# How many steps of projections stand between a normalised q or k tile and its transposes

## The chip, the cores and the metric

The kernel runs on one core of one Trainium2 chip. The metric is the device time of one execution in microseconds (us), taken as the median over several runs. The profile and the trace are of one such execution; its span runs from its first to its last instruction.

## What is computed

One decoder layer on 512 tokens of width 1024, in float32. Cut to what matters here:

```
h = rms_norm(x) * (1 + scale(c)) + shift(c)
proj = h @ w_in
(q_a, k_a, v_a, z_a, q_b, kc, vc, ks, vs, kw, vw, z_b, g_b) = split(proj)
qa, ka       = qk_norm(q_a) * qscale, qk_norm(k_a)
o_a          = sliding-window attention (window 128, sinks, bias), 8 heads, 2 kv heads
qb           = qk_norm(q_b) * qscale
k_cmp, v_cmp = two-layer MLP over overlapping blocks of kc, vc (k_cmp then qk-normed)
o_cmp        = softmax attention of qb on the compressed k_cmp, v_cmp
o_sel, o_win = attention of qb on qk_norm(ks), vs and on qk_norm(kw), vw, with bias
o_b          = gates * (o_cmp, o_sel, o_win), summed
y            = concat(o_a * silu(z_a), o_b * silu(z_b)) @ w_out ;  out = x + gate(c) * y
```

## The kernel before

TensorE works in float32 parts: a matrix is split into a high part and the rest (`wh`, `wl`; `hh`, `hl`), and a product of two matrices is three matmuls per contraction chunk. Heads are taken in pairs r = 0 to 3, one head of each of the two kv groups. Kind "a" is the sliding-window group, kind "b" the sparse one.

Two lines of work are interleaved from about 60 us on.

The first is `run()`, a list of slots of attention. A slot is one head pair, one branch and one block of 128 queries; there are 16 slots of kind a and then 28 of kind b. At turn t, `run()` writes the transposes of slot t-2 (`slot_trans`, L974 or L984), the scaling of slot t-1 (`slot_scale`), the scores of slot t (`slot_scores`, L923, or L896 for the slot that takes both branches of the first block), and, once a head pair is complete, its products with v (`slot_pv`, L1001). On TensorE these stand in blocks (`with block()`) that keep the order of the text among themselves.

The second is a stream of projections, a Python generator (`gen1`, then `gen2`). Each step of a unit writes three matmuls, for one contraction chunk (L503 in `unit_nat`, L513 in `unit_col`), and then yields a cost. `run()` draws steps from it by a budget of 3.6 us per turn for kind a (`PER_A`), half ahead of `slot_pv` and half behind it. Of the projections of kind b that matter here: the selected keys and values (`kv_sel`), the window's (`kv_win_g`), the queries in two halves (`q_b0`, `q_b1`, 96 matmuls each) and the gates' z units of 24 matmuls, z0 to z7.

What follows a projection is written as a small generator of its own and put in the list `posts`. `with_posts` takes one step of the first generator in that list after each step of projections. So a `yield 0.0` in such a generator puts one step of projections, three matmuls, between what is written before it and what is written after it. The generators that the change touches:

- `post_k(ty, kr)` normalises the keys of the selected (ty 1) and the window branch (ty 2): squares and sums, the eight small VectorE operations of `rsqrt`, and then `k_scale`: two VectorE multiplications into `kn` (L569, L571), two yields, four transposes into a PSUM tile `pt` (L576), and the copies and subtractions that split the transposed keys (L581, L582).
- `post_q(qr, half)` does the same for a half of the queries: sums (L542), `rsqrt`, and for each of its two head pairs `q_scale`: a multiplication into `qn` (L551), `Q_LEAD` = 3 yields, four transposes into `pt` (L557), two copies on ScalarE (L562) and two subtractions on VectorE (L563). Below, q0 to q3 are the four head pairs of kind b; q0 and q1 come from the first half, q2 and q3 from the second.

The keys of kind a (ty 0) and the queries of kind a go through the same two functions.

In `posts`, the keys of the selected branch stand ahead of `cmp_mlp`, the MLP of the compressed branch, whose first half of products (L630) is written by a step of it, and whose second half is written by `run()` at the next `slot_pv` (`jobs`). Its later steps hold a transpose of hidden values (L652), the second layer (L663, L666) and a transpose of the compressed keys `kcn` (L683). `cmp_attn` (L699 and on) comes after the queries and needs all four head pairs of them; its products stand in a block as well. `post_z` follows each z unit.

The text is not the order on an engine. The framework's planner goes through the text with its own estimates of durations, and gives each engine, at each moment, the earliest instruction of the text that it believes to be ready by then and that has room for its tile. The order so found is fixed in the program, and each engine then waits wherever an instruction is not ready.

Of the kernel before, what the change touches and what calls it, by code (L numbers as in the profile page):

```python
# [36 lines left out]
Q_LEAD = 3  # L37


def rev(ap):  # L40

    dims = [list(e) for e in ap.ap]
    step, n = dims[-1]
    dims[-1] = [-step, n]
    return bass.AP(tensor=ap.tensor, offset=ap.offset + step * (n - 1), ap=dims)
# [37 lines left out]
def hybrid_layer_kernel(ctx, tc, A, out):  # L83
# [11 lines left out]
    def T2(dt, name):  # L95
        return t2.tile([128, S], dt, name=name, tag="t2")
# [385 lines left out]
    def W2(name, shape=(128, 512)):  # L482
        return mp.tile(list(shape), F32, name=name, tag="w2", bufs=5)

    def PT():
        return ps_t.tile([128, 512], F32, name="pt")
# [48 lines left out]
    def sumsq(dst, src, nblk, on_act):  # L535
        sq = W2("sq")[:, 0:nblk * HD]
        if on_act:
            ACT.activation(sq.rearrange("p (a b) -> p a b", a=src.shape[1]) if len(src.shape) == 3 else sq,
                           src, AF.Square)
        else:  # L540
            POOL.tensor_tensor(sq, src, src, op=OP.mult)
        DVE.tensor_reduce(dst, sq.rearrange("p (b d) -> p b d", d=HD), AX.X, OP.add)  # L542

    def rnorm(ssq, n):
        DVE.tensor_scalar(ssq, ssq, 1.0 / HD, EPS, op0=OP.mult, op1=OP.add)
        return rsqrt(ssq, n)

    def q_scale(src, rn, heads):

        qn = W2("qn", (128, 8, HD))  # L550
        DVE.tensor_tensor(qn.rearrange("p (t h) d -> p t h d", t=NB), src,  # L551
                          rn[:, :, :, None].to_broadcast([128, NB, 2, HD]), op=OP.mult)
        for _ in range(Q_LEAD):
            yield 0.0
        pt = PT()
        for tb in range(NB):
            PE.transpose(pt[:, tb * 128:(tb + 1) * 128], qn[:, 2 * tb:2 * tb + 2].rearrange("p h d -> p (h d)"), ident)  # L557
        view = lambda ap: ap.rearrange("p (t q) -> p t q", t=NB)
        for n, h in enumerate(heads):
            qs[h] = T2(F32R, f"qs{h}")  # L560
            own, other = slice(64 * n, 64 * n + 64), slice(64 - 64 * n, 128 - 64 * n)
            ACT.activation(view(qs[h][own]), rev(view(pt[own])), AF.Copy)  # L562
            DVE.tensor_tensor(view(qs[h][other]), rev(view(pt[own])), view(qs[h][own]).bitcast(F32), op=OP.subtract)  # L563
        yield 0.44

    def k_scale(ty, src, rn):

        kn = W2("kn", (128, 8, HD))
        DVE.tensor_tensor(kn, src.rearrange("p t (g d) -> p (t g) d", d=HD), rn[:, :, None].to_broadcast([128, 8, HD]),  # L569
                          op=OP.mult)  # L570
        DVE.tensor_tensor(kn, kn, kg[:, ty:ty + 1, :].to_broadcast([128, 8, HD]), op=OP.mult)  # L571
        for _ in range(2):
            yield 0.0
        pt = PT()
        for t in range(NB):
            PE.transpose(pt[:, t * 128:(t + 1) * 128], kn[:, 2 * t:2 * t + 2].rearrange("p g d -> p (g d)"), ident)  # L576
        for g in range(2):
            own = slice(64 * g, 64 * g + 64)
            high = kT[ty, g][own, 0, :]
            for part in (own, slice(64 - 64 * g, 128 - 64 * g)):  # L580
                ACT.activation(kT[ty, g][part, 0, :], pt[own, :], AF.Copy)  # L581
                DVE.tensor_tensor(kT[ty, g][part, 1, :], pt[own, :], high.bitcast(F32), op=OP.subtract)  # L582
        yield 0.44
# [3 lines left out]
    def prep_a():  # L587
        ss = sm.tile([128, 40], F32, name="ss_a")
        for tb in range(NB):
            DVE.tensor_reduce(ss[:, 8 * tb:8 * tb + 8], qsq[tb].rearrange("p (b d) -> p b d", d=HD), AX.X, OP.add)  # L590
        DVE.tensor_reduce(ss[:, 32:40], ksq.rearrange("p t (g d) -> p (t g) d", d=HD), AX.X, OP.add)
        rn = rn_a[0] = rnorm(ss, 40)
        yield 0.0
        yield from k_scale(0, kraw, rn[:, 32:40])
        yield from prep_q_a(0)

    def prep_q_a(r):
        pair = lambda ap: ap.rearrange("p (t g r) -> p t g r", t=NB, g=2)[:, :, :, r]
        q4 = qraw.rearrange("p t (g r d) -> p t g r d", g=2, r=4)
        yield from q_scale(q4[:, :, :, r], pair(rn_a[0][:, 0:32]), (r, 4 + r))  # L600
# [176 lines left out]
    def post_k(ty, kr):  # L777
        ss = sm.tile([128, 8], F32, name="ss_k")
        sumsq(ss, kr.rearrange("p t n -> p (t n)"), 8, True)
        rn = rnorm(ss, 8)  # L780
        yield from k_scale(ty, kr, rn)
# [10 lines left out]
    def post_q(qr, half):  # L792

        ss = sm.tile([128, 16], F32, name="ss_q")
        for p in range(2):
            sumsq(ss[:, 8 * p:8 * p + 8], qr[:, 2 * p:2 * p + 2].rearrange("p t n -> p (t n)"), 8, True)
        yield 0.0
        rn = rnorm(ss, 16).rearrange("p (t h) -> p t h", t=NB)
        for j in range(2):
            r = 2 * half + j  # L800
            yield from q_scale(qr[:, :, 128 * j:128 * j + 128].rearrange("p t (g d) -> p t g d", g=2),
                               rn[:, :, 2 * j:2 * j + 2], (8 + r, 12 + r))

    def gen1():
        for _ in range(2):
# [23 lines left out]
        for half in range(2):  # L829
            qr = mp.tile([128, NB, 256], F32, name="pp", bufs=3)  # L830
            for p in range(2):
                b = PJ()
                yield from with_posts(unit_nat(f"q_b{half}", (2 * p, 2 * p + 1), 256, b))
                ACT.activation(qr[:, 2 * p:2 * p + 2, :], b.rearrange("p (t n) -> p t n", t=2), AF.Copy)
            posts.insert(0, post_q(qr, half))
# [318 lines left out]
```

## Time and profile before

| | us |
|---|---|
| median of 3 runs (lowest to highest) | 306.42 (305.98 to 307.14) |
| the profiled execution, its own time | 306.31 |
| its span | 304.2 |
| TensorE matmuls busy | 296.2 (97%) |
| TensorE weight loads busy | 251.6 (83%) |
| VectorE (DVE) busy | 238.3 (78%) |
| ScalarE (ACT) busy | 195.3 (64%) |

Times inside the execution are counted from the start of its span, so its own time is 2.1 us above the span. In a row of the timeline stand the start, the duration, the engine, the line of the kernel, the operation with what it writes and reads, and how many instructions the row joins; a wait ahead of it stands in brackets with what ended it. Matmuls overlap: one of 256 columns shows 0.28 us, but the next one starts 0.12 us after it. So a hold of TensorE is read from starts, not from busy time.

### The profile page before, as it was taken

To read this page: it belongs to the slowest core of one execution; us is meant where nothing else is said; L and a number is where in the kernel's file an instruction comes from. 1 tells how busy PE (TensorE), PEld (TensorE's weight loads), DVE (VectorE), ACT (ScalarE), POOL (GpSimd) and SP (SyncE) were. 2 spreads that over 40 slices of the span, in tenths; PEclk is the share of its full clock that TensorE was granted. 3 is DMA by queue.
4 is the path that set the end of the run, shared out by engine and by line. 5 is a ranking of instruction groups with operands and counts; after the bars stand their busy time and mean duration, and the time that the engine had idled before them with its cause. 6 is when DMAs were issued, how large, how long until landed. Compare 5 with 4: busy or idle time off the path is not lost.

```text
span 304.2 us, 5822 instructions
## 1 busy us (share of the span) xinstructions
PE 296.2 (97%) x2118; PEld 251.6 (83%) x2119; DVE 238.3 (78%) x669; ACT 195.3 (64%) x474; POOL 3.8 (1%) x26
## 2 busy tenths in 40 slices
PE   7899999999999999989999999999999999999995
PEld 3677888889999999989887688788878888787885
DVE  4889996999985596877899999999985985819211
ACT  4876547777886578859666767776866875824000
POOL 1000000000000000000000000000000000000000
PEclk9999999999999999999999999999999999999999
DMA  7999947887225960320682023236100000105301
GB/s 276 375 375 408 354 178 246 270 271 264 83 93 165 354 211 2 111 62 9 225 285 72 1 79 130 82 127 199 46 1 2 0 2 1 37 0 180 132 34 69
DMA packets 27419, 44.20 MB, mean 145 GB/s; under 512 B 1712, under 2 KB 19408, under 8 KB 27392
## 3 DMA queue, kind: packets, MB, share of 16 engines
q1 hardware_dynamic: 27392, 43.84, 42.4%
q8 instruction: 16, 0.26, 0.3%
q14 instruction: 11, 0.09, 0.1%
HBM read 41.70 MB, written 2.14 MB: 144 GB/s over the span
## 4 chain that ended last, share of the span: by engine, by line
PE 74%; DVE 12%; ACT 8%; DMA 3%; issue 2%; SPq 1%; POOL 0%; ACTq 0%; POOLq 0%
PE pj L513 28%; PE sq L299 8%; PE po L1001 8%; PE pj L503 6%; PE s L923 6%; PE skv L300 4%; PE pt L984 4%; PE pt L974 3%; DMA ada_ring<-in_w_ada_ss 3%; PE s L630 2%; ACT pa L938 2%; DVE wl L181 2%; DVE qs L563 1%; ACT wh L180 1%; DVE pa L931 1%
## 5 line engine op out<-in xcount | busy, mean ns | idle before, releaser
L503 PE MATMUL pj<-wh,hh 128*128 128x256 f32 (+1 forms) x128 | 36.9, 288 | 0.0
L181 DVE TENSOR_TENSOR wl<-raw,wh 128x512 fp32r<-128x512 f32 (+1 forms) x52 | 35.4, 690 | 1.4 <-PE pj L503 0.8
L503 PE MATMUL pj<-wl,hh 128*128 128x256 f32 (+1 forms) x128 | 36.5, 285 | 0.0
L503 PE MATMUL pj<-wh,hl 128*128 128x256 f32 (+1 forms) x128 | 36.4, 285 | 0.0
L180 ACT ACTIVATE wh<-raw 128x512 fp32r<-128x512 f32 (+1 forms) x52 | 31.1, 636 | 6.7 <-PE pj L513 4.4
L938 ACT ACTIVATE pp<-pp,nm 128x256 f32<-128x256 f32 (+2 forms) x48 | 29.3, 612 | 7.8 <-DVE nm L931 7.7
L513 PE MATMUL pj<-hh,wl 128*128 128x512 f32 x80 | 32.3, 404 | 0.0
L513 PE MATMUL pj<-hh,wh 128*128 128x512 f32 x80 | 32.1, 401 | 0.0
L513 PE MATMUL pj<-hl,wh 128*128 128x512 f32 x80 | 31.7, 396 | 0.0
L931 DVE CUSTOM_DVE_ANT_0 pp<-s,bias 128x256 f32<-128x256 f32 (+2 forms) x48 | 25.6, 552 | 4.0 <-PE s L923 3.7
L513 PE MATMUL pj<-yh,wl 128*128 128x512 f32 (+1 forms) x72 | 26.8, 373 | 0.0
L513 PE MATMUL pj<-yl,wh 128*128 128x512 f32 (+1 forms) x72 | 26.7, 371 | 0.0
L513 PE MATMUL pj<-yh,wh 128*128 128x512 f32 (+1 forms) x72 | 26.4, 371 | 0.0
L503 PEld LDWEIGHTS pj<-wl,hh 128*128 128x128 f32 x128 | 24.1, 189 | 0.4 <-issue 0.3
L503 PEld LDWEIGHTS pj<-wh,hh 128*128 128x128 f32 x128 | 24.1, 188 | 0.4 <-issue 0.3
L503 PEld LDWEIGHTS pj<-wh,hl 128*128 128x128 f32 x128 | 24.1, 188 | 0.0
L923 PE MATMUL s<-kTb,qs 128*128 128x256 f32 (+2 forms) x96 | 23.7, 359 | 0.0
L959 DVE TENSOR_SCALAR pp<-pp,rr,grev 128x256 f32<-128x256 f32 (+2 forms) x48 | 21.0, 476 | 0.5
L1080 DVE SCALAR_TENSOR_TENSOR fin<-pj,gate_lsb,xr 128x512 f32<-128x512 f32 (+1 forms) x9 | 6.2, 690 | 16.1 <-PE pj L513 16.1
L985 ACT COPY ptT<-pt 128x384 f32<-128x384 f32 (+1 forms) x32 | 15.7, 529 | 3.3 <-PE pt L984 3.3
L513 PEld LDWEIGHTS pj<-hl,wh 128*128 128x128 f32 x80 | 15.0, 188 | 3.2
L513 PEld LDWEIGHTS pj<-hh,wl 128*128 128x128 f32 x80 | 15.1, 189 | 2.9
(246 smaller groups left out, 703.5 us busy)
## 6 DMA issues: line engine op xcount, KB each, us to landing
ada_ring<-in_w_ada_ss SPq DMA_DIRECT2D x16, 512.0 KB, 9.7
raw<-in_w_cmp SPq DMA_DIRECT2D x8, 512.0 KB, 5.4
raw<-in_w_gate SPq DMA_DIRECT2D x8, 512.0 KB, 6.4
raw<-in_w_o SPq DMA_DIRECT2D x8, 512.0 KB, 3.8
wst_ring<-in_w_qkv_a SPq DMA_DIRECT2D x8, 384.0 KB, 9.4
bias<-line_d SPq DMA_DIRECT2D x8, 256.0 KB, 4.5
xr<-in_xT SPq DMA_DIRECT2D x8, 256.0 KB, 4.2
raw<-in_w_q_b SPq DMA_DIRECT2D x4, 512.0 KB, 5.6
```

Of the source, the lines that this page charges most:

```text
L180: ACT.activation(wh, src, AF.Copy)
L181: DVE.tensor_tensor(wl, src, wh.bitcast(F32), op=OP.subtract)
L299: PE.matmul(pj_q[tb], lt, w[:, 0:512], start=f, stop=l, skip_group_check=True)
L300: PE.matmul(pj_kv[tb // 2][:, tb % 2, :], lt, w[:, 512:768], start=f and tb % 2 == 0, stop=l, skip_group_check=True)
L503: PE.matmul(bank[:, t * n:(t + 1) * n], h[:, tb * 128:(tb + 1) * 128], w[:, k % 2, :], start=k == 0 and m == 0, stop=k == 7 and m == 2)
L513: PE.matmul(bank, w, h[:, cols], start=k == 0 and m == 0, stop=k == 7 and m == 2)
L923: PE.matmul(ps[g], qs[h][:, 128 * i:128 * i + 128], kT[br, g][:, hl_, lo:lo + n], start=hl_ == 0, stop=hl_ == 1)
L931: DVE.tensor_tensor_reduce(out=P[:, g, 0:w], in0=ps[g][:, 0:w], in1=bt, scale=1.0, scalar=init, op0=OP.add, op1=OP.min, accum_out=nm[:, g: ...
L938: ACT.activation(P[:, g, 0:e], P[:, g, 0:e], AF.Exp, bias=nm[:, g:g + 1], scale=-1.0, accum_out=dn[:, g:g + 1])
L959: DVE.tensor_scalar(v, v, rr[:, g:g + 1], gates[:, g, br:br + 1], op0=OP.mult, op1=OP.mult)
L985: ACT.copy(T[:, 0:nb, :], rev(pt[:, 0:nb * 128].rearrange("p (b q) -> p b q", b=nb)))
L1001: PE.matmul(o[64 * g:64 * g + 64, 128 * i:128 * i + 128], vb[:, 64 * g:64 * g + 64], sl["T"][g][:, b, :], start=first_of and b == 0, stop= ...
```

## The change

`q_scale` gets its number of yields as an argument. `post_q` gives it `Q_LEAD * (2 - j)`: six for the first head pair of each half (q0 and q2) and three, as before, for the second. In `k_scale` the number becomes four for the two key tiles of kind b and stays two for kind a. The queries of kind a keep three.

```diff
-    def q_scale(src, rn, heads):
+    def q_scale(src, rn, heads, lead=Q_LEAD):
...
-        for _ in range(Q_LEAD):
+        for _ in range(lead):
             yield 0.0
         pt = PT()
...
-        for _ in range(2):
+        for _ in range(4 if ty else 2):
             yield 0.0
         pt = PT()
...
             yield from q_scale(qr[:, :, 128 * j:128 * j + 128].rearrange("p t (g d) -> p t g d", g=2),
-                               rn[:, :, 2 * j:2 * j + 2], (8 + r, 12 + r))
+                               rn[:, :, 2 * j:2 * j + 2], (8 + r, 12 + r),
+                               Q_LEAD * (2 - j))
```

No instruction is added or removed. The second head pair of a half comes after the first in the same generator, so all that follows q0 or q2 in it moves by three steps; all that follows the selected keys in `posts`, `cmp_mlp` first, moves by two.

## The prediction

> **What bounds the kernel now.** I read the page first, then the windows, then the waits of TensorE, then its timeline around each of the transposes that move. The page gives the span and who carries the chain that ended last.
>
> ```profile
> span 304.2 us, 5822 instructions
> ...
> PE 74%; DVE 12%; ACT 8%; DMA 3%; issue 2%; SPq 1%; POOL 0%; ACTq 0%; POOLq 0%
> ```
>
> Three windows in the stretch that the change touches; the columns are the length, then busy time and count of PE, PEld, DVE, ACT and POOL, the granted clock, the DMA share and GB/s.
>
> ```profile
> 130.00:140.00 10.00, 8.83 (x80) 8.52 (x80) 8.34 (x25) 6.52 (x17) 0.38 (x2) 1.00 0.09 33
> 150.00:160.00 10.00, 9.88 (x56) 8.14 (x55) 9.63 (x33) 5.32 (x17) 0.00 (x0) 1.00 0.77 262
> 170.00:200.00 30.00, 29.91 (x160) 24.58 (x159) 29.18 (x86) 22.13 (x54) 0.00 (x0) 1.00 0.27 89
> ```
>
> PE is full nearly everywhere, at a granted clock of 1.00; 130 to 140 is the exception, with 1.17 us idle. From 150 on DVE is nearly full too. The waits of PE, all together, name one wait on a q tile:
>
> ```profile
> PE pt L557 <- DVE qn L551: 1.2, 1, 1.2
> ```
>
> In the timeline of PE that wait stands at q0.
>
> ```profile
> 130.47 0.28 PE L503 MATMUL pj<-wl,hh 128*128 128x256 f32 x1
> 130.59 0.28 PE L503 MATMUL pj<-wh,hl 128*128 128x256 f32 x1
> 132.04 0.63 PE L557 MATMUL pt<-first,qn 128*128 128x128 f32 x4 [1.17 <-DVE qn L551]
> 132.42 0.37 PE L503 MATMUL pj<-wh,hh 128*128 128x256 f32 x1
> 132.62 0.60 PE L557 MATMUL pt<-first,qn 128*128 128x128 f32 x4
> 133.06 0.60 PE L974 MATMUL pt<-first,pa 128*128 128x128 f32 x4
> ```
>
> Matmuls start 0.12 us apart; from 130.59 to 132.04 it is 1.45, so 1.33 us of PE is lost. As PE carries 74% of the chain, a lost microsecond here counts nearly whole. The other moved transposes, k1 and k2 (selected, window) and q2 and q3, and that of `kcn`, stand here:
>
> ```profile
> 89.85 0.29 PE L503 MATMUL pj<-wh,hl 128*128 128x280 f32 x1
> 89.98 0.29 PE L503 MATMUL pj<-wh,hh 128*128 128x280 f32 x1
> 90.40 0.63 PE L576 MATMUL pt<-first,kn 128*128 128x128 f32 x4
> 90.86 0.38 PE L974 MATMUL pt<-first,pa 128*128 128x128 f32 x2
> ...
> 108.39 0.33 PE L683 MATMUL pt<-first,kcn 128*128 128x128 f32 x1
> 108.55 0.60 PE L974 MATMUL pt<-first,pa 128*128 128x128 f32 x4
> ...
> 152.43 0.39 PE L513 MATMUL pj<-hh,wh 128*128 128x512 f32 x1
> 152.66 0.40 PE L513 MATMUL pj<-hl,wh 128*128 128x512 f32 x1
> 153.18 0.66 PE L557 MATMUL pt<-first,qn 128*128 128x128 f32 x4
> 153.67 0.60 PE L974 MATMUL pt<-first,pa 128*128 128x128 f32 x4
> 154.03 0.72 PE L896 MATMUL s<-kTb,qs 128*128 128x256 f32 x4
> 154.59 0.60 PE L557 MATMUL pt<-first,qn 128*128 128x128 f32 x4
> ```
>
> At k1 PE loses 0.42 less 0.13, so 0.29 us; at q2 0.52 less 0.23, again 0.29. These three holds, 1.91 us, are all that later transposes of k1, q0 and q2 could win on PE.
>
> **Where the transposes stand, in the text and in the program.** This decides the case. The windows below begin with the first matmul of a unit and end at the transposes; the count in brackets is that of the projections' matmuls in between: `kv_win_g` ahead of k1, `q_b0` ahead of k2, `q_b1` ahead of q0, z0 ahead of q2.
>
> ```profile
> 80.03:90.30 10.27, 8.41 (x61) 1.00 0.40 128
> 106.42:114.20 7.78, 4.76 (x38) 1.00 0.64 208
> 125.32:131.00 5.68, 4.80 (x39) 1.00 0.69 209
> 144.00:153.00 9.00, 8.95 (x38) 1.00 0.66 216
> ```
>
> Now the places in the text, three matmuls a step. k1: `kn` in step 1 and two yields, so transposes in step 3, behind 9 matmuls; with four yields behind 15. k2: the gates take steps 1 and 2, so behind 15, after the change 21. q0: sums in step 1, `qn` in step 2, three yields, so step 5 and 15 matmuls; with six yields step 8 and 24. q1: `qn` in the step after q0's transposes, three yields, so 27, then 36. q2 as q0: 15, then 24. q3: 33, then 42, as `post_z` of z0 takes two steps in between.
>
> So the program does not have them where the text has them: 61 against 9 at k1, 38 against 15 at k2, 39 against 15 at q0, 38 against 15 at q2. The planner had already put them at the point at which it believed them ready, 23 to 52 matmuls later. The new places, 15, 21, 24 and 24, are still earlier than that. The longer lead is a lower bound that was overrun already, and should move none of these four. The 1.33 us at q0 is then an error of the planner's estimate, not a short lead: it believed `qn` ready at about 130.7, and DVE ended it at 131.9 (1.29 us for two of them from 131.20, so 0.65 for the first).
>
> ```profile
> 126.76 0.57 ACT L834 ACTIVATE pp<-pj 128x512 f32<-128x512 f32 x1
> ...
> 131.20 1.29 DVE L551 TENSOR_TENSOR qn<-pp,n_y 128x512 f32<-128x512 f32 x2
> ...
> 134.69 1.41 DVE L563 TENSOR_TENSOR qs<-pt,qs 64x512 fp32r<-64x512 f32 x2
> ```
>
> The chain from the copy of the projection (126.76) to `qn` is untouched by the edit. I cost q0, k1, k2 and q2 at 0.
>
> **What the change does move.** First, q3: its place was behind 38 matmuls (none stands between q2's and q3's transposes) and may not be earlier than 42 now. Four matmuls at 0.23 us (152.43 to 152.66) make it 0.9 us later. Nobody on PE waits for q3 before `cmp_attn`, priced below. q1's place, 40, stays allowed (36).
>
> Second, slot blocks pass transposes. Behind k1, `kcn`, q1 and q2 a slot's transposes (L974) start at once (90.86, 108.55, 133.06, 153.67), in every case a slot written later than the transposes ahead of it. I read this as slots held in text order behind late transposes. With about 11 steps a turn (3.6 us at 0.33 us of cost), turn 13 is written behind 30 matmuls of `q_b1`, turn 16 behind 15 to 18 of z0, turn 17 behind 33. Before, q1 (27), q2 (15) and q3 (33) were written ahead of these turns; after, they come behind them (36, 24, 42). `kcn` likewise falls behind turn 7. So four blocks of transposes and scores stop waiting for a transpose written after them: turn 13 by the 0.44 us of q1's transposes (132.62 to 133.06); turn 16 by up to 20 matmuls of z0 (38 less 18), 4.7 us; turns 7 and 17 something between. For PE this is an exchange, a block earlier and projections later, and worth 0 by itself. But their VectorE and ScalarE work starts earlier, in front of a stretch in which DVE is 97% busy (29.18 of 30). The bounds: no gain, and the removal of the small holds that PE still has at slot transposes in the stretch behind, for which q2's 0.29 is the nearest row; six slots so held would be 1.7 us. I take one such hold, 0.3 us, since PE is at 29.91 of 30 there and shows little to win.
>
> Third, the loads. `cmp_mlp` calls eight loads on SP's queue with its products, two steps later in the text (6 matmuls of 0.13 us, 0.8 us). The products stood in the program behind k1 and its slot, after 61 matmuls of `kv_win_g`; their new text place, 13 steps or 39 matmuls, is still earlier, so the loads go out when they did. Cost 0; without that cover 0.8 us of lateness on a queue that moves 33 GB/s in 130 to 140. The first half of the products must be written before the `slot_pv` of head pair 0, as the second half is written there: it was step 11 of `kv_win_g` and is now step 13, and that half turn draws to step 14 or so. It fits by one step; if it did not, the second half would come four turns later.
>
> The sum, against the profiled execution's own 306.31: 0 for q0, k1, k2, q2; 0 for q3; -0.3 for the slots: **306.0 us**. The median of the runs, 306.42, is 0.1 above the profiled execution, less than their spread.
>
> **The rivals.** (1) The planner moves the transposes along with the text: its readiness shifts by as much as the lead, and the holds at k1, q0 and q2 go. Then 306.31 - 1.91 = **304.4**, with the slots' 0.3 even 304.1. For it: the hold at q0 is real and is the largest of PE in the touched stretch. Against it: the counts, 39 against 24.
>
> (2) Slower, at `cmp_attn`. Its products need q3's last subtraction, and they stood behind it with room:
>
> ```profile
> 162.95 0.69 DVE L563 TENSOR_TENSOR qs<-pt,qs 64x512 fp32r<-64x512 f32 x1
> ...
> 167.44 1.06 PE L699 MATMUL s<-qs,kTc 128*32 128x512 f32 x8
> ```
>
> That is 163.64 to 167.44, 3.8 us. Now q3 is written behind two slots and z0's post, and DVE is full there (9.63 of 10). If the planner puts L699 where it believes q3 ready, its error decides. At q0 that error was 1.33 us on a chain of 5.1 (126.76 to 131.9), a quarter; q3's chain from its transposes to its last subtraction is 9.05 us (154.59 to 163.64), a quarter of it 2.4 us, with PE and all slot blocks behind it held. Then 306.0 + 2.4 = **308.4**. It decides from the point at which L699 is next on PE before q3's last subtraction has ended; 3.8 us of room, and nine matmuls by which L699 also moves in the text, speak against it.
>
> (3) A hold for want of a PSUM bank. The pool of `pt` names two banks; q0's is read until the subtractions that start at 134.69 (1.41 us for two), so up to 136.1. If the slot transposes had to wait for it behind 133.06, up to 3.0 us could go: **309.0**. Against it: at 133.06 a third `pt` tile was written while q0's and q1's were still unread. The Trainium skill, in Perfetto Trace Analysis under Optimization Strategy, says that one gap that repeats on the engine that should be full can mean that PSUM or SBUF lacks room for the next tile. By that rule the holds at k1, q0 and q2 would be one shortage, and slots closer to the q transposes would make it worse, to this rival's 309.0. The trace disagrees at 133.06, and names `qn`, not a reader of `pt`, as what ended the hold.
>
> **How the numbers follow.** Half a per cent is 1.5 us, about what a measurement of this kernel can tell from no change. The main case, the holds stay and the slots bring 0 to 1.7 us, gets 0.62, of which 0.04 lies below 304.8. Rival 1 gets 0.20, all faster; rival 2 gets 0.14 and rival 3 0.04, all slower. So faster 0.24, the same 0.58, slower 0.18. The range runs from rival 1 with a little on top, 304.1, to two thirds of rival 2's price with the slots' gain lost, 306.3 + 1.6 = 307.9. The main case alone: 304.6, all of the 1.7 won, to 306.9, nothing won and two new holds like k1's.
>
> **What would show it.** Right: in the trace after, q0's transposes stand behind 39 matmuls of `q_b1`, give or take 3, with a hold on `qn` of 1 us or more; k1 and k2 behind about 61 and 38; L974 and L896 of turns 16 and 17 come ahead of q2 and q3; q3 stands behind 42 or more of z0. Wrong: q0 without a hold, or behind fewer or many more matmuls; a new wait of PE on L563 at L699; a wait of L974 on a reader of `pt`. What would make it wrong most easily is that a small shift of the text makes the planner arrange the stretch from 100 us on anew, as its errors, and so the holds, then fall elsewhere.

## The result and the profile after

| | us |
|---|---|
| after, median of 11 runs (lowest to highest) | 308.46 (307.12 to 308.95) |
| before, median of 11 runs beside them | 306.07 (305.71 to 307.14) |
| ratio | 1.0072 [1.0057, 1.0087] |
| profiled execution of after, its span | 308.59, 306.5 |

The change makes the kernel slower by 0.72%, some 2.2 us. The forecast was no change, 306.0, with a range that ended at 307.9. In the kernel after, the lines up to 801 keep their numbers and those behind are one higher (L1002 is L1001 of before). The page gives the span and the chain that ended last.

```profile
span 306.5 us, 5856 instructions
...
PE 60%; DVE 23%; DMA 7%; ACT 5%; issue 2%; SPq 2%
```

TensorE carried 74% of that chain and carries 60% now; VectorE and DMA have taken the rest. So something outside TensorE has got onto the path. The waits of PE say where.

```profile
PE pt L576 <- DVE kn L571: 1.1, 2, 0.9
PE po L1002 <- DVE nm L932: 1.0, 1, 1.0
PE pt L557 <- DVE qn L551: 0.8, 1, 0.8
...
PE s L924 <- ACT kT L581: 0.4, 1, 0.4
```

The third line is the hold at q0, known from before and even smaller. The longer of the two waits in the first line and the wait in the second make up most of the loss, and neither stands at an instruction that the edit moves. The first of them in the timeline of PE, before and then after:

```profile
61.14 0.40 PE L513 MATMUL pj<-hh,wl 128*128 128x512 f32 x1
61.39 0.66 PE L576 MATMUL pt<-first,kn 128*128 128x128 f32 x4
```

```profile
61.43 0.40 PE L513 MATMUL pj<-hh,wl 128*128 128x512 f32 x1
62.76 0.33 PE L576 MATMUL pt<-first,kn 128*128 128x128 f32 x1 [0.94 <-DVE kn L571]
```

These are the transposes of kind a's keys, whose two yields the edit leaves alone. Before, they stood 0.25 us behind the matmul ahead of them, now 1.33. So 1.1 us is lost at 62 us, and the order of instructions is the same in both programs, on every engine that computes, up to about 101 us. A delay that comes ahead of the first instruction in another order can't come from the order. It leads back through `kn` and ScalarE to a load. The queue of SP, the engine that issues the loads, first before and then after; the duration of a pair reaches to the end of its second issue:

```profile
35.93 0.33 SPq L429 DMA_DIRECT2D rest<-in_rest  x1
36.35 9.94 SPq L161 DMA_DIRECT2D raw<-in_w_kv_cmp  x2
```

```profile
43.04 0.33 SPq L429 DMA_DIRECT2D rest<-in_rest  x1
43.46 3.13 SPq L161 DMA_DIRECT2D raw<-in_w_kv_cmp  x2
```

The load of `rest` (480 KB of small constants) goes out 7.1 us later. What it waits for is in the list of waits of that queue, and what comes of it on ScalarE in the timeline:

```profile
SPq L429 <- DVE xTp L283: 6.2, 1, 6.2
```

```profile
51.92 1.67 ACT L180 ACTIVATE wh<-raw 128x512 fp32r<-128x512 f32 x3 [1.10 <-DMA raw<-in_w_kv_cmp]
```

L283 is the last scaling of the input by `rb`. `rest` and `rb` have nothing to do with each other in the kernel's text, but the framework places all tiles in SBUF by itself from their lifetimes. In the built program after, `rest` lies at bytes 114464 to 119328 of a partition and `rb` at 114464 to 116512. `rest` had the same place before; it is `rb` that has moved, from byte 189408, and before no tile of that time shared the place of `rest`. So the load must wait for the last reader of `rb`, and the load of `kv_cmp` queued behind it waits too. ScalarE splits that weight (L180) ahead of the copies from which `kn` is made. Before, the same three splits began without a wait:

```profile
50.47 1.66 ACT L180 ACTIVATE wh<-raw 128x512 fp32r<-128x512 f32 x3
```

The second loss is at the first product with v of head pair b0. PE after, and then DVE after:

```profile
203.68 0.94 PE L924 MATMUL s<-kTb,qs 128*128 128x384 f32 x4
204.47 0.40 PE L513 MATMUL pj<-hh,wl 128*128 128x512 f32 x1
205.89 0.44 PE L1002 MATMUL po<-ptT,vs 128*64 128x128 f32 x4 [1.03 <-DVE nm L932]
```

```profile
203.44 1.26 DVE L248 CUSTOM_DVE_ANT_0 raw<-raw,scb,first 128x1024 f32<-128x1024 f32 x1
...
204.63 0.73 DVE L960 TENSOR_SCALAR pp<-pp,rr,grev 128x256 f32<-128x256 f32 x2
205.28 0.55 DVE L932 CUSTOM_DVE_ANT_0 pp<-s,bias 128x384 f32<-128x384 f32 x1
```

In both programs `po` of b0 is put into the PSUM bank of the first of the two score tiles written just ahead of it, so its first matmul waits until VectorE has read those scores (L932). After, the planner has a row sum for the gate (L248, 1.26 us, needed only at the end of the kernel) and a slot's scaling on VectorE ahead of that read, and one projection matmul on TensorE to cover it. Before, three matmuls stood there on PE, and on VectorE the read came ahead of the row sum. PE before, and then DVE before:

```profile
201.16 0.95 PE L923 MATMUL s<-kTb,qs 128*128 128x384 f32 x4
...
202.42 0.40 PE L513 MATMUL pj<-hl,wh 128*128 128x512 f32 x1
202.74 0.44 PE L1001 MATMUL po<-ptT,vs 128*64 128x128 f32 x4
```

```profile
201.79 0.56 DVE L931 CUSTOM_DVE_ANT_0 pp<-s,bias 128x384 f32<-128x384 f32 x1
...
203.46 1.28 DVE L248 CUSTOM_DVE_ANT_0 raw<-raw,scb,first 128x1024 f32<-128x1024 f32 x1
```

### The profile page after: what moved, and what is told of

Read it like the earlier page. It is cut to its first block, busy times and chain, and to the rows that moved or that the text cites. A ratio compares the mean times of both kernels' runs of the same rounds, so it can differ in the third digit from the quotient of the medians.

```text
span 306.5 us, 5856 instructions
## 1 busy us (share of the span) xinstructions
PE 296.8 (97%) x2119; PEld 252.1 (82%) x2119; DVE 238.5 (78%) x669; ACT 197.1 (64%) x474; POOL 4.6 (1%) x26
## 4 chain that ended last, share of the span: by engine, by line
PE 60%; DVE 23%; DMA 7%; ACT 5%; issue 2%; SPq 2%
PE pj L513 26%; PE po L1002 8%; PE s L924 7%; PE pj L503 6%; DVE ada_ring L248 4%; PE pt L985 4%; DMA wst_ring<-in_w_qkv_a 4%; PE pt L975 3%; DVE wl L181 3%; PE s L630 2%; DMA raw<-in_w_kv_cmp 2%; DVE swl L278 2%; DVE pa L932 1%; DMA ada_ring<-in_w_ada_ss 1%; ACT wh L180 1%
## 5 line engine op out<-in xcount | busy, mean ns | idle before, releaser
L180 ACT ACTIVATE wh<-raw 128x512 fp32r<-128x512 f32 (+1 forms) x52 | 31.9, 639 | 19.0 <-PE pj L513 13.7
L513 PE MATMUL pj<-hl,wh 128*128 128x512 f32 x80 | 32.1, 401 | 0.0
L513 PE MATMUL pj<-hh,wl 128*128 128x512 f32 x80 | 31.9, 399 | 0.0
L513 PE MATMUL pj<-hh,wh 128*128 128x512 f32 x80 | 31.9, 398 | 0.0
L932 DVE CUSTOM_DVE_ANT_0 pp<-s,bias 128x256 f32<-128x256 f32 (+2 forms) x48 | 25.5, 551 | 3.1 <-PE s L924 3.0
L513 PE MATMUL pj<-yl,wh 128*128 128x512 f32 (+1 forms) x72 | 26.9, 374 | 0.0
L513 PE MATMUL pj<-yh,wl 128*128 128x512 f32 (+1 forms) x72 | 26.7, 371 | 0.0
L513 PE MATMUL pj<-yh,wh 128*128 128x512 f32 (+1 forms) x72 | 26.2, 370 | 0.0
L513 PEld LDWEIGHTS pj<-hh,wh 128*128 128x128 f32 x80 | 15.0, 188 | 3.1 <-ACT qraw L472 0.2
L513 PEld LDWEIGHTS pj<-hh,wl 128*128 128x128 f32 x80 | 15.0, 188 | 3.1
L513 PEld LDWEIGHTS pj<-hl,wh 128*128 128x128 f32 x80 | 15.1, 188 | 2.9 <-issue 0.2
```

The source lines that it names most:

```text
L180: ACT.activation(wh, src, AF.Copy)
L513: PE.matmul(bank, w, h[:, cols], start=k == 0 and m == 0, stop=k == 7 and m == 2)
L932: DVE.tensor_tensor_reduce(out=P[:, g, 0:w], in0=ps[g][:, 0:w], in1=bt, scale=1.0, scalar=init, op0=OP.add, op1=OP.min, accum_out=nm[:, g: ...
```

## The experiments

Theory L: the loss is a new SBUF layout (the late load) plus the new order on VectorE at b0. Rival T: the longer leads, and the order that they make, cost it. Rival C: the hold at b0 is a consequence of something else, and taking it away brings nothing. Ratios below are to the kernel before, timed beside each run (305.7 to 305.9 us).

**Taking away the shared place, and splitting the change.** The first three runs have one edit in common, which keeps `rest` alive from the start:

```diff
     rest = con.tile([128, 1216], F32, name="rest")
+    POOL.memset(rest[:, 0:1], 0.0)
```

In the file the write stands on the line above it, behind a semicolon, so in the kernels below the lines keep the numbers of before (L1001, not L1002). The whole change with it:

> The change as it stands, and one write of zeros into a column of `rest` by GpSimd at the start, so that no early tile can share the place of `rest` in SBUF. TensorE, VectorE and ScalarE get the same instructions in the same order as after the change; only what the load of `rest` (L429) waits for differs. Theory L (the layout: `rest` was put over `rb`, so its load and the loads of `kv_cmp` behind it on SP's queue went out 7.1 us later): the load goes out at about 36 instead of 43.04, the transposes of kind a's keys come at 61.4 to 61.7 instead of 62.76, and the time falls by 1.1 to 1.4 us, from 308.46 to 307.1 to 307.4; the hold of 1.03 us at L1001 (b0) stays, since the order is the same. Rival T (the longer leads and their order cost it all): 308.4, no change. Rival C (the hold at b0 is only a consequence of the early delay): both go, 306.1.

Measured: 306.90 us, ratio 1.0035 [1.0020, 1.0050].

```profile
35.73 0.33 SPq L429 DMA_DIRECT2D rest<-in_rest  x1
```

```profile
PE po L1001 <- DVE nm L931: 1.1, 1, 1.1
```

The queue of SP has the load back at 35.7 and PE's waits still have the hold at b0. By PE's timeline the transposes of kind a's keys stand at 61.56. 0.37%, 1.1 us, is won with the same order on PE, VectorE and ScalarE. T falls for this half.

The two parts of the change alone, `4 if ty else 2` in `k_scale` and `Q_LEAD * (2 - j)` in `post_q`:

> The keys' part of the change alone (four steps for the two key tiles of kind b; the queries keep three and three), with `rest` written early as in the run before, so that its place is not shared. The order differs from before only in 51 matmuls between k2's projections and `cmp_mlp`. Theory L: nothing is lost, 306.1 (305.8 to 306.5). Rival T, if the keys' order carries the loss: 307.2 or more, with a shift that begins between 85 and 125 us.

Measured: 305.19 us, 0.9978 [0.9967, 0.9990]. Not only is nothing lost, 0.6 to 0.7 us is won against before, which no theory had; this median is the lowest of the study.

> The queries' part alone (six steps for q0 and q2), with `rest` written early so that its place is not shared. Theory L: no loss up to 190 us; the hold at L1001 of head pair b0 belongs to the order that this part makes, so about 1.0 us is lost there: 307.1 (306.8 to 307.4). Rival T: 308.4, the whole loss. Rival C: 306.1, no hold at b0.

Measured: 307.10 us, 1.0040 [1.0026, 1.0054], with the hold of 1.0 at L1001. As L had it.

> The queries' part alone without that early write; here the load of `rest` again waits for VectorE, as after the change. TensorE, VectorE and ScalarE have the same order as in the run before (queries alone, kept apart). Theory L: 1.1 to 1.4 us above that run, about 308.4, the difference made before 63 us. Rival T: the same time as that run.

Measured: 308.50 us, 1.0077 [1.0059, 1.0095], 0.37% above the run before. The load goes out at 42.3. By the ratios the price of the shared place is the same 1.1 us in two pairs of equal order.

**Making the load late by hand.** The best kernel so far, the keys' part with `rest` apart, gets the wait back without any shared place. `LW` moves the load two steps later in the text, behind the second write:

```diff
-LW = 4
+LW = 6
...
             DVE.tensor_tensor(y[k][:, c], xT[k][:, c], by[:, c], op=OP.mult)
+            k == 7 and DVE.memset(rest[:, 0:1], 0.0)
```

> The keys' part alone with `rest` apart, and a second write of zeros into a column of `rest`, by VectorE right behind the last scaling by `rb` (L283), ahead of the load in the text (which moves from step 3 to step 5 of the first stage for that). All engines keep the order of the keys' part alone; only the load of `rest` waits for that write, so it goes out at about 42.7 instead of 35.4, as after the change. Theory L: the lateness alone costs 1.1 us: 306.3 (306.0 to 306.6) against 305.19 of the keys' part apart, made at kind a's key transposes, 61.3 to about 62.4. Rival (the late load is only a companion of something else in the new layout): 305.2, no difference.

Measured: 306.25 us, 1.0010 [0.9997, 1.0023], so 1.06 us above 305.19 (0.98 by the ratios). PE shows the same wait at the same place as after the change:

```profile
61.81 0.66 PE L576 MATMUL pt<-first,kn 128*128 128x128 f32 x4 [0.91 <-DVE kn L571]
```

With that write some 2 us earlier on VectorE, behind L292 for chunk 5, and so the load at 39.67:

> The same with the second write behind the high-low split of chunk 5 (L292), so that the load of `rest` goes out at about 40 instead of 35.4. After the change the loads of `kv_cmp` were 7.1 us late and ScalarE waited 1.1 us for them beyond a moved chain of its own, so theory L has some 5 to 6 us of room: 4.5 us of lateness cost nothing, 305.2 (304.9 to 305.5). Rival (each microsecond of lateness costs its share, 1.1 for 7.1): 305.9.

Measured: 305.38 us, 0.9976 [0.9965, 0.9987]. Against the load of the keys' part (35.43), 4.3 us of lateness cost nothing that can be told from noise, and 6.5 us (41.95; 7.2 if counted against TensorE, which ran 0.7 us earlier in that execution) cost 1.06: it isn't a price per microsecond but a room that runs out. The windows show where; the last two columns are the DMA share and GB/s, first in the kernel before, then with the load at 41.95.

```profile
36.00:43.00 7.00, 7.00 (x43) 6.13 (x42) 6.93 (x14) 4.29 (x8) 0.00 (x0) 1.00 0.82 279
46.00:52.00 6.00, 6.00 (x33) 5.01 (x32) 3.48 (x6) 4.29 (x8) 0.00 (x0) 1.00 0.75 225
```

```profile
36.00:43.00 7.00, 7.00 (x42) 6.13 (x41) 6.96 (x12) 4.85 (x8) 0.00 (x0) 1.00 0.37 127
46.00:52.00 6.00, 6.00 (x34) 5.17 (x33) 2.44 (x4) 3.21 (x6) 0.00 (x0) 1.00 0.93 313
```

The second load of `kv_cmp` waits for a place of its own and is not late: it goes out at 45.74 before and at 44.95 here. What the late load does is move `rest` and the first half of `kv_cmp`, 992 KB, out of a stretch at 0.82. The larger part goes into 43 to 46 us, where nothing was moved before (0 GB/s, 256 here), and the rest falls behind 46 us, where the DMA engines go to 0.93 against 0.75 before and 0.78 with the load at 39.67. ScalarE then waits for both halves: 0.85 us ahead of the first split (L180), at 47.80, and 1.17 us ahead of the next three, at 50.97, which began at 50.40 without a wait when the load stood at 39.67. That the fuller stretch is what delays the second half is read from these rows; no run changed it alone.

**Other leads.** Five steps for q0 and q2 in place of six, keys four, `rest` apart:

> Queries with five steps for q0 and q2 instead of six, keys with four, `rest` apart. In this program six matmuls of projections and more stand on TensorE between the last scores of b0 and its first product with v, where six steps leave one; the piece of the gate's row sum (L248, 1.27 us) comes on VectorE behind the first reduction of those scores instead of ahead of it. Theory L (the hold of 1.03 us at L1001 is the price of that order): no hold at L1001 of b0, and about 0.9 us below the change with `rest` apart (306.9): 306.0 (305.5 to 306.4). Rival C (the longer lead of the queries costs by itself, or the fuller SBUF places of `wh` cost it): 306.9 or more, without a hold at L1001.

Measured: 308.90 us, 1.0091 [1.0071, 1.0110]. A miss. The hold at b0 did go down to 0.2, but a new one stands behind the last head pair:

```profile
275.62 0.39 PE L1007 MATMUL po<-ptc,vc_low 128*128 128x512 f32 x1
277.45 0.73 PE L513 MATMUL pj<-yh,wh 128*128 128x512 f32 x2 [1.44 <-ACT yh L860]
```

The matmuls of projections that cover b0 there are missing later. Their counts (L513) from 200 to 240 and from 240 to 276 us, first with six steps and then with five:

```profile
200.00:240.00 40.00, 16.25 (x59) 1.00 0.14 47
240.00:276.00 36.00, 15.27 (x56) 1.00 0.01 2
```

```profile
200.00:240.00 40.00, 18.26 (x69) 1.00 0.07 23
240.00:276.00 36.00, 12.53 (x46) 1.00 0.01 2
```

Ten are used earlier, and nothing is left to cover the split of the last head pair's output (`yh`). The profiled execution of this run took 308.08; what the median has above that, this trace doesn't show. So this run doesn't tell L from C.

A shorter lead, one step for q0 and q2:

> A shorter lead: one step for q0 and q2 instead of three, keys with two as before. In this program the load of `rest` waits for VectorE, and VectorE has the gate's row sum (L248) ahead of the reduction of b0's last scores, both as after the change. Theory L (the loss is the new layout and the order at b0, whatever the lead): 1.1 to 1.6 us lost before 66 us and about 1 us at L1001: 308.5 (307.8 to 309.2). Rival T (it is the longer lead that costs, a shorter one costs nothing or wins): 306.1 or below.

Measured: 310.17 us, 1.0141 [1.0116, 1.0166], still above the range that L gave. The load goes out at 43.0, the waits at L576 (0.9) and at L1001 (1.0) are both there, and ScalarE waits 1.93 us for `kv_cmp` instead of 1.10; what more is lost between 155 and 208 us was not followed up. Making the lead shorter brings both of the losses that making it longer brings. It is not the length that costs.

**The hold at b0 by itself.** The change with `rest` apart, and one gate row sum over 128 columns in place of 1024, which leaves out 7/8 of it; the order is that of the change with `rest` apart on every engine.

```diff
-            row_sum(raws[key], prm[:, 16 + n:17 + n], gate[:, n:n + 1])
+            w_ = raws[key][:, 0:128] if n == 5 else raws[key]
+            DVE.tensor_tensor_reduce(out=w_, in0=w_, in1=scb[:, 0:w_.shape[-1]], scale=1.0,
+                                     scalar=prm[:, 16 + n:17 + n], op0=OP.mult, op1=OP.add,
+                                     accum_out=gate[:, n:n + 1])
```

> The change with `rest` apart (306.9), every engine in the same order; only the gate's row sum for chunk 5, which stands on VectorE ahead of the reduction of b0's last scores (from 202.22, 1.27 us), is made over 128 of its 1024 columns, so 7/8 of that sum is left out. Theory L (L1001 of b0 waits for the bank of those scores, and so for what VectorE has queued ahead of their reduction): the hold falls from 1.1 to about 0.2 us and the time by 0.8 to 0.9, to 306.0 (305.7 to 306.4). Rival C (the hold only stands where something else would stop TensorE anyway, or VectorE is the bound there): 306.7 or more.

Measured: 306.11 us, 1.0006 [0.9991, 1.0021].

The timeline of DVE, then of PE, in this run:

```profile
202.03 0.33 DVE L755 CUSTOM_DVE_ANT_0 raw<-raw,scb,first 128x128 f32<-128x128 f32 x1
...
202.29 0.73 DVE L959 TENSOR_SCALAR pp<-pp,rr,grev 128x256 f32<-128x256 f32 x2
202.94 0.55 DVE L931 CUSTOM_DVE_ANT_0 pp<-s,bias 128x384 f32<-128x384 f32 x1
```

```profile
203.04 0.40 PE L513 MATMUL pj<-hh,wl 128*128 128x512 f32 x1
203.55 0.44 PE L1001 MATMUL po<-ptT,vs 128*64 128x128 f32 x4
```

The control has `n == 7` in place of `n == 5`:

> The control: the same order again, and the same 7/8 left out of the gate's row sum for chunk 7, which stands on VectorE behind that reduction (from 207.49, 1.27 us). Theory L: it is ahead of nothing that TensorE waits for, the hold of 1.1 us at L1001 stays, 306.9 (306.6 to 307.2). Rival C (VectorE is the bound there): 0.8 us or more below 306.9, as in the run before.

Measured: 307.02 us, 1.0034 [1.0020, 1.0048], hold 1.04. The same 0.9 us of VectorE work taken out: 0.8 us won where it stands ahead of the reduction, nothing where it stands a few instructions behind it. C falls.

Against the kernel before the sum closes: 0.72% lost by the change, 0.37% of it the shared place (1.0072 to 1.0035), 0.29% the gate's row sum (1.0035 to 1.0006), and 0.06% [-0.09, 0.21] is left. That so little is left is in part luck, as two things cancel. The keys' part alone stands at 0.9978, so against it the kernel with both losses taken out (1.0006) is still 0.28%, about 0.9 us, slower. The traces show where it starts. The keys' part and the change with `rest` apart have the same order on PE, VectorE and ScalarE up to 147 us, and by then PE is 0.83 us later in the second: 0.24 from 47 us on, 0.43 at one product of scores (L923), the rest in small steps. First the keys' part, then the change with `rest` apart:

```profile
68.45 0.38 PE L923 MATMUL s<-kT,qs 128*128 128x256 f32 x1
```

```profile
69.13 0.39 PE L923 MATMUL s<-kT,qs 128*128 128x256 f32 x1 [0.43 <-ACT kT L581]
```

Up to there the two programs differ in the places of tiles and in the waits that these bring, so the shared place of `rest` is not the whole price of the new layout. Which other places make these 0.8 us is not shown.

## Why the prediction was wrong

**Where the transposes stand: right at k1, q0, q2 and q3, wrong at k2.** The counts ahead of k1, k2 and q0 in the kernel after, from the first matmul of their units, and that ahead of q3:

```profile
81.80:92.15 10.35, 8.38 (x61) 1.00 0.55 176
109.25:118.40 9.15, 6.91 (x56) 1.00 0.49 149
127.36:133.60 6.24, 4.79 (x39) 1.00 0.75 250
```

```profile
145.80:158.50 12.70, 10.66 (x44) 1.00 0.74 230
```

61 and 39 as before, 44 at q3 (42 or more was said), and in the same stretch 37 at q2, which had 38. k2 went from 38 to 56: that the longer lead "should move none of these four" did not hold there. The hold at k2 itself is only 0.18 us. The hold at q0 stayed, 0.82 in the trace and 1.10 less 0.12, so 0.98, from starts, where 1 or more was said.

**Slots pass ahead: right as an order.** L975 of turn 16 stands at 150.00, ahead of q2's transposes at 155.39. That this brings 0.3 us was not seen by itself; with both losses taken out nothing is left in which to see it.

**Loads, cost 0: right for the eight loads named, and the failed step.** The products that call the eight (L630) begin at 93.45 in place of 91.65, so 1.8 us later, as k1's transposes just ahead of them do (92.20 and 90.40). But the price of the edit was summed over what the edit moves. It also moved lifetimes of tiles, and with them the places of tiles that the edit doesn't touch; one load of 480 KB got a wait by it, at 43 us, nearly 60 us ahead of the first instruction that stands in another order. The sum had no term for it, and it measured 1.1 us. The runs put that load's room between 4.3 and 6.5 us of lateness; that it would lose its room could not be read from the profile of before.

**The second failed step** is the cost of 0 for all that lies behind the moved transposes. "A small shift of the text makes the planner arrange the stretch from 100 us on anew" was named as the likeliest way to be wrong, without a price, and the range gave it none. It was so: from the queries' part alone came a VectorE order in which a gate sum stood ahead of b0's reduction, 0.8 us by the run that shortened it.

**The rivals.** (1) The planner moves the transposes with the text: no, by the counts; k2 moved, but by 18 matmuls where the text moved by 6. (2) A hold at L699: no. It began at 171.21, and q3's last subtraction had ended at 165.04:

```profile
164.35 0.69 DVE L563 TENSOR_TENSOR qs<-pt,qs 64x512 fp32r<-64x512 f32 x1
```

(3) A PSUM bank: not at `pt`, where it was looked for, but 70 us later at `po`, as one gap of 1.03 us. The Trainium skill's sentence on consistent bubbles (Perfetto Trace Analysis, Optimization Strategy) speaks of a gap that repeats; the trace agrees with it on the cause, a bank not yet free, and not on the form, as this gap came once.

**What the keys' part won.** k1 and k2 were costed at 0; alone and with `rest` apart they win 0.5 to 0.7 us in two kernels (0.9978 and 0.9976). A part can be read: two small VectorE operations of a slot (L955, L963) stood inside the chain of `rsqrt` that leads to `qn`, and stand ahead of it now. First before, then keys alone:

```profile
129.54 0.17 DVE L955 RECIPROCAL rr<-dn 128x2 f32<-128x2 f32 x1
...
131.20 1.29 DVE L551 TENSOR_TENSOR qn<-pp,n_y 128x512 f32<-128x512 f32 x2
```

```profile
129.01 0.16 DVE L955 RECIPROCAL rr<-dn 128x2 f32<-128x2 f32 x1
...
130.88 1.29 DVE L551 TENSOR_TENSOR qn<-pp,n_y 128x512 f32<-128x512 f32 x2
```

`qn` starts 0.32 us earlier, and the wait at q0 is 0.84 in place of 1.17. The hold at q0 is thus shortened by the edit at the keys and not by the longer lead at q0. It is 0.8 to 0.9 in all the kernels with four steps for the keys and 1.2 in those with two. The rest is for the most part not the keys' doing. PE in the keys-alone run is 0.20 us behind before at 40 us and 0.22 ahead at 101 us (L652 at 101.22 and 101.44), and up to there both programs have the same order. So 0.4 us comes without any change of order, with the layout that has `rest` apart. From there to 120 us, the stretch of k2, 0.24 us goes again (120.13 and 120.11), and then comes the win at q0; from 101 us to the end the new order wins some 0.2 us on balance. No run has the kernel before with that one write alone, so the two shares are read from the traces and not shown by a time.

**What stays open.** The 0.8 us that the change with `rest` apart has lost to the keys' part by 147 us. In the programs with six, five or one step for the queries, the wait of 0.4 us for `kT` at L923 is there in every one, and ScalarE's splits of weights wait more for TensorE (13.7 us in 12 waits after, 4.4 us in 4 before), as their `wh` tiles share places. That the one makes the other is not shown: the keys' part alone has 9.0 us in 6 such waits and loses nothing at L923. No run took these waits away.

## What to carry to other kernels

Where a framework places tiles and orders instructions by itself, an edit of a few yields is also a new memory layout and a new order far from the edit. So compare first where the two traces part: a shift that begins ahead of the first instruction in another order is a matter of places or loads, and one write that keeps a tile alive from the start told it apart here without touching the order on TensorE, VectorE and ScalarE. Such a write makes a new layout of its own, so it wants a twin: the unchanged kernel with the same write, which this study lacks. And look at each engine's queue ahead of whatever frees a PSUM bank for the bounding engine: work that is needed only at the end of the kernel costs its full length there and nothing a few instructions later.

## What the runs showed of the hardware that was not expected

A load that went out 4.3 us late cost nothing and one 6.5 us late cost 1.06 us: the room ended where transfers fell together with the next loads, with the DMA engines from 46 to 52 us at 0.93 and 313 GB/s, against 0.78 and 246 with the load 4.3 us late and 0.75 and 225 before. And VectorE, busy for 9.73 of the 10 us around the hold at b0 in the change with `rest` apart, was not the bound there:

```profile
196.00:206.00 10.00, 8.72 (x66) 6.94 (x66) 9.73 (x34) 6.74 (x21) 0.00 (x0) 1.00 0.58 182
```

0.9 us less work on it changed the time by 0.8 us or by nothing, depending on which side of one reduction that work stood.
